# Prompt attention scores with their sign turned and read from pairs of PSUM banks

## The chip, the cores and the metric

The kernel runs on one core of one Trainium2 chip. The metric is the device time of one execution in microseconds; before the change it is 2411.74 us (median of 3 runs, 2409.42 to 2413.18). The core's engines each run their own queue in a fixed order: TensorE (PE; its weight loads are shown apart as PEld), VectorE (DVE), ScalarE (ACT), GpSimd (POOL) and SyncE (SP), which issues most transfers.

## The reference, cut to what matters

The reference is a two-layer encoder step. Layer 0 runs latent attention (8 heads) and a state-space layer side by side, layer 1 is a gated convolution. The change concerns the attention of the prompt alone: 2048 tokens, 16 blocks of 128 queries, and a mask by chunks of 64 tokens.

```python
q_n = rms_norm(q[..., :NOPE_DIM], g_q_nope)                 # 64 columns, scaled by the norm weight
q_r = rope(rms_norm(q[..., NOPE_DIM:], g_q_rope), pos)      # 32 columns
s = (einsum('bqhd,bkhd->bhqk', q_n, k_n) + einsum('bqhr,bkr->bhqk', q_r, k_r)) * ATTN_SCALE
s = where(mask, s, -1e30)        # key chunk <= query chunk
p = softmax(s, axis=-1)
return einsum('bhqk,bkhd->bqhd', p, v)
```

ATTN_SCALE is 96 to the power -0.5; the kernel calls it ATT.

## The kernel before

The program has four stages, one after the other: input projections with the state-space scan (`phase_a`), queries, keys and values with the sample's attention (`phase_b`), the prompt's attention (`phase_c`), and the output projection with layer 1 (`phase_d`). All matmuls that need precision are done in three passes on split operands (high part and low part: `qh`, `ql`, `kh`, `kl`).

In `phase_b`, `p_tr` transposes normalised queries on TensorE; ScalarE copies them out of PSUM (line 702) and multiplies each of the 96 rows by a column `g_qn2`. Its first 64 rows hold the norm weight (times 8, line 445), the other 32 rows hold ones. The result goes to DRAM as `s_qT` and is loaded again per head in `phase_c`.

`phase_c` has 128 steps: 8 heads, and per head 16 blocks `b` of 128 queries. Block `b` sees nk = 128(b+1) keys. A step has these parts:

- **Scores** (`scores`): the keys are cut into chunks of up to 512 columns. Each chunk is three matmuls into one PSUM bank `s_ps` (lines 1301 to 1303). The mask comes in by 16 extra rows of `kh` and `qh`, which add -1e30 to masked scores. VectorE then reads the bank once (line 1304): it copies the scores to SBUF (`s_sb`, or `s_sm` up to 1024 keys) and takes the running maximum of the row, which each following read of the step takes as its operand. The profile shows each read as two rows, the read and a `DVE_READ_ACCUMULATOR`, which writes the maximum.
- **Softmax**: after the last chunk VectorE multiplies the maximum by -ATT (line 1307), ScalarE takes exp(ATT x score + that bias) in one or two pieces and sums (line 1315), VectorE adds the two sums and takes the reciprocal (1318, 1319), GpSimd scales the row (1323).
- **Transposition** (`trans`): groups of up to four 128x128 transpositions fill one PSUM bank `pt` (line 1342); ScalarE copies the bank to `pth` (1351), VectorE writes the rest to `ptl` (1352), and the bank is free.
- **Output** (`av`): per 128 keys two matmuls, with `pth` and `ptl`, into a bank `o` (1362, 1363); after two pairs of blocks `fin` gates and stores the result.

PSUM has eight banks: in this stage two for `o`, three for `pt`, three for `s_ps` (lines 1244 to 1246).

The order of the work is first written out by hand: each piece gets a time by a plan (`cum`, `spread`, lines 1388 to 1460), with scores 8 units ahead of transpositions, and pieces are emitted in order of these times. The context of line 2013 is opened with `schedule_with_timeline_sim=True`; it lays down each engine's order before the run, and this order is not the emitted one: in the trace TensorE takes a transposition of the first step before the second score chunk of the sixth, which was emitted earlier. On the chip the order is fixed, and each engine waits where its next instruction isn't ready.

Of the kernel before, what the change touches and what calls it, by code (L numbers as in the profile page):

```python
# [10 lines left out]
F32 = mybir.dt.float32  # L11
# [3 lines left out]
AF = mybir.ActivationFunctionType  # L15
OP = mybir.AluOpType
# [9 lines left out]
ATT = (64 + 32) ** -0.5  # L26
# [3 lines left out]
PSUM = bass.MemoryType.PSUM  # L30
# [6 lines left out]
def f(ap):  # L37
    return ap.bitcast(F32)
# [22 lines left out]
class K:  # L61
# [362 lines left out]
    def phase_b(self):  # L424
        nc, A, S = self.nc, self.A, self.S
        tt = nc.vector.tensor_tensor
        act = nc.scalar.activation
        with ExitStack() as es:
# [3 lines left out]
            pt = self.pool(es, "b_pt", 2, PSUM)  # L432
            ps = self.s5p
# [8 lines left out]
            for nm, r in (("g_kn2", 128), ("g_qn2", 64), ("g_q64", 128)):  # L442
                t = cp.tile([128, 1], F32, name=nm)
                nc.sync.dma_start(t, A[nm])
                nc.gpsimd.tensor_scalar(t[:r], t[:r], 8.0, 1.0, op0=OP.mult, op1=OP.mult)
                setattr(self, nm, t)
            e3 = cp.tile([128, G, 24], F32, name="e3")
            nc.gpsimd.memset(e3, 64 * EPS)
# [190 lines left out]
            with ExitStack() as e2:  # L639
# [4 lines left out]
                box, nm = {}, {}  # L644
# [593 lines left out]
    def phase_c(self):  # L1238
        nc, A, S = self.nc, self.A, self.S
        with ExitStack() as es:  # L1240
# [1 line left out]
            sp = self.pool(es, "c_s", 2)  # L1242
            kps = (self.kx, self.pool(es, "c_k", 1))
            po = self.pool(es, "c_po", 2, PSUM)
            pt = self.pool(es, "c_pt", 3, PSUM)
            ps = self.pool(es, "c_ps", 3, PSUM)
            hd = {}
            kq = [{nm: kp.tile([112 if nm[1] == "h" else 96, TP], F32R, name=nm) for nm in ("kl", "ql", "kh", "qh")} for kp in kps]
            eye = self.ident[96:112, 96:112][:, :, None].to_broadcast([16, 16, 64])
            for t in kq:  # L1250
                for nm, at, val in (("kh", 1, -1e30), ("qh", 0, 1.0)):
                    r = t[nm][96:112].rearrange("p (b e t) -> p b e t", e=2, t=64)
                    nc.gpsimd.tensor_scalar(r[:, :, at], eye, val, 1.0, op0=OP.mult, op1=OP.mult)
                    nc.gpsimd.tensor_scalar(r[:, :, 1 - at], eye, 0.0, 1.0, op0=OP.mult, op1=OP.mult)
# [27 lines left out]
            def halves(h, nm, c0, first=False):  # L1282
# [4 lines left out]
                else:  # L1287
                    nc.gpsimd.tensor_scalar(hi, f(lo), 1.0, 1.0, op0=OP.mult, op1=OP.mult)
                    nc.gpsimd.tensor_tensor(lo, f(lo), f(hi), op=OP.subtract)

            def scores(h, b):
                t = hd[h]
                nk = 128 * (b + 1)
                sb = sp.tile([128, TP if nk > 1024 else 1024], F32, name="s_sb" if nk > 1024 else "s_sm", bufs=4)
                st = sp.tile([128, 16], F32, name="s_st", bufs=6)
                q = slice(b * 128, b * 128 + 128)
                items = []

                def chunk(i, k0, n, last):
                    o = ps.tile([128, 512], F32, name="s_ps")  # L1300
                    nc.tensor.matmul(o[:, :n], t["qh"][:, q], t["kh"][:, k0:k0 + n], start=True, stop=False)  # L1301
                    nc.tensor.matmul(o[:, :n], t["ql"][:, q], t["kh"][:96, k0:k0 + n], start=False, stop=False)  # L1302
                    nc.tensor.matmul(o[:, :n], t["qh"][:96, q], t["kl"][:, k0:k0 + n], start=False, stop=True)  # L1303
                    nc.vector.tensor_scalar(sb[:, k0:k0 + n], o[:, :n], 1.0, st[:, i - 1:i] if i else None,  # L1304
                                            op0=OP.mult, op1=OP.max, accum_out=st[:, i:i + 1])
                    if last:
                        nc.vector.tensor_scalar(st[:, 5:6], st[:, i:i + 1], -ATT, None, op0=OP.mult)  # L1307
                        e0 = 0
                        parts = []
                        while e0 < nk:  # L1310
                            m = nk - e0
                            m = m if m <= 1024 else 1024 if m > 1152 else 640
                            j = 8 + len(parts)
                            parts.append(j)
                            nc.scalar.activation(sb[:, e0:e0 + m], sb[:, e0:e0 + m], AF.Exp, bias=st[:, 5:6], scale=ATT, accum_out=st[:, j:j + 1])  # L1315
                            e0 += m
                        if len(parts) == 2:
                            nc.vector.tensor_tensor(st[:, 8:9], st[:, 8:9], st[:, 9:10], op=OP.add)
                        nc.vector.reciprocal(st[:, 7:8], st[:, 8:9])  # L1319
                        e0 = 0  # L1320
                        while e0 < nk:
                            m = min(1024, nk - e0)
                            nc.gpsimd.tensor_scalar(sb[:, e0:e0 + m], sb[:, e0:e0 + m], st[:, 7:8], 1.0, op0=OP.mult, op1=OP.mult)  # L1323
                            e0 += m

                k0, i = 0, 0
                while k0 < nk:
                    n = nk - k0
                    if n > 512:
                        n = 384 if n == 640 else 512  # L1330
                    items.append((0.42 * n / 512 * 1.55, lambda i=i, k0=k0, n=n, l=k0 + n == nk: chunk(i, k0, n, l)))
                    k0 += n
                    i += 1
                return sb, items

            def trans(b, sb, pth, ptl):
# [72 lines left out]
                return run  # L1409

            def nchunks(b):
                nk, n = 128 * (b + 1), 0
                while nk > 0:
                    nk -= nk if nk <= 512 else 384 if nk == 640 else 512
                    n += 1
                return n

            def mk_s(n):
                h, a, b = steps[n]

                def make():
                    st_["sb", n], items = scores(h, b)
                    return items
                return make
# [26 lines left out]
            for n, (h, a, b) in enumerate(steps):  # L1451
                t0, t1 = cum[n], cum[n + 1]
                if n % 16 == 0:
                    add(cum[max(0, n - 14)] - LEAD - 4 if n else -1e9, lambda h=h: load(h))
                    if n:
                        spread(cum[n - 9] - LEAD, cum[n - 2] - LEAD, 8, lambda i, h=h: halves(h, "kq"[i % 2], 512 * (i // 2)))
                spread(t0 - LEAD - (t1 - t0), t0 - LEAD, nchunks(b), sub(("S", n), mk_s(n)))
                spread(t0, t1, (b + 4) // 4, sub(("T", n), mk_t(n)))
                if b % 2 == 1:
                    spread(t1 + AVD, t1 + AVD + (t1 - cum[n - 1]), 2 * a + 2, sub(("A", n), mk_a(n, (n // 2) % 2, None)))  # L1460
# [568 lines left out]
```

## Time and profile before

| what | us |
|---|---|
| median of 3 runs | 2411.74 |
| the profiled execution | 2409.65 |
| its span in the trace | 2407.9 |
| PE, busy in the span | 2228.1 (93%) |
| PEld | 2006.6 (83%) |
| DVE | 1834.1 (76%) |
| POOL | 1427.4 (59%) |
| ACT | 1177.0 (49%) |

An engine is busy while an instruction of it runs; starts of the next may lie under the end of one. The span runs from the first to the last instruction of the trace. The prompt's attention lies in the middle of it, from about 0.9 to 1.4 ms. "Idle before, releaser" says what ended the time in which an engine stood still; a wait of PEld is a wait before a weight load, which is the first instruction of a matmul.

### The profile page before, as it was taken

How to read it: one execution, taken by the hardware profiler on the slowest of the kernel's cores; microseconds unless marked ns; L12 is line 12 of the kernel's file. 1: busy time of each engine (PE TensorE's matmuls, PEld its weight loads, DVE VectorE, ACT ScalarE, POOL GpSimd, SP SyncE). 2: the span in 40 equal slices, each digit the busy share in tenths (PEclk: the TensorE clock that was granted, in tenths of full speed). 3: DMA queues.
4: the chain of work that ended last, by engine and by line, in shares of the span. 5: the costliest groups of instructions: out<-in, count | busy, mean ns of one | idle time of the engine just before them, and what ended most of it. 6: DMA issues, size and time to landing. Idle time of an engine off the chain costs nothing.

```text
span 2407.9 us, 39063 instructions
## 1 busy us (share of the span) xinstructions
PE 2228.1 (93%) x13471; PEld 2006.6 (83%) x13471; DVE 1834.1 (76%) x3995; ACT 1177.0 (49%) x2226; POOL 1427.4 (59%) x1328
## 2 busy tenths in 40 slices
PE   6798989998889987999999989999999999999996
PEld 6798989996648876888888888988888789989996
DVE  7763246985456666888889945999998999999984
ACT  4343346235436765777777743433433533533423
POOL 5232543216265666777777534686778888976851
PEclk9999999999989987999999999999999999999998
DMA  8886574315637772222222356755355245443552
GB/s 193 200 222 160 133 187 148 93 49 167 198 109 217 229 238 78 71 65 72 71 73 67 97 198 201 245 180 166 120 171 172 85 140 206 153 141 121 159 166 86
DMA packets 289670, 352.08 MB, mean 146 GB/s; under 512 B 79936, under 2 KB 231808, under 8 KB 288960
## 3 DMA queue, kind: packets, MB, share of 16 engines
q1 hardware_dynamic: 288768, 348.40, 48.8%
q8 instruction: 107, 1.75, 0.3%
q10 hardware_dynamic: 704, 1.18, 0.2%
q14 instruction: 91, 0.75, 0.1%
HBM read 255.72 MB, written 93.52 MB: 145 GB/s over the span
## 4 chain that ended last, share of the span: by engine, by line
PE 50%; DVE 6%; POOL 2%; ACT 2%; DMA 2%; issue 1%; SPq 0%; POOLq 0%; DVEq 0%; ACTq 0%
PE pp L71 12%; PE pp L72 12%; PE pp L73 12%; PE pt L1342 4%; PE o L1363 2%; PE o L1362 2%; PE s_ps L1301 2%; PE s_ps L1302 2%; PE s_ps L1303 2%; DVE acc L1652 1%; DVE s_sb L1304 1%; DVE ptl L1352 1%; ACT s_sb L1315 1%; DMA b1l<-s_mx_l 1%; DMA ql<-s_qT 1%
## 5 line engine op out<-in xcount | busy, mean ns | idle before, releaser
L1652 DVE SCALAR_TENSOR_TENSOR acc<-vt,cw,acc 128x384 f32<-128x384 f32 (+2 forms) x1142 | 670.0, 659 | 2.5 <-ACT acc L1638 1.3
L1848 POOL TENSOR_TENSOR wl<-wr,wh 128x1024 fp32r<-128x1024 f32 x110 | 265.7, 2417 | 113.3 <-ACT wh L1847 112.3
L1847 ACT ACTIVATE wh<-wr 128x1024 fp32r<-128x1024 f32 x136 | 144.1, 1060 | 327.8 <-PE pp L72 161.9
L1352 DVE TENSOR_TENSOR ptl<-pt,pth 128x512 fp32r<-128x512 f32 (+2 forms) x320 | 184.3, 601 | 20.1 <-ACT pth L1351 18.7
L1351 ACT ACTIVATE pth<-pt 128x512 fp32r<-128x512 f32 (+2 forms) x320 | 158.7, 527 | 67.3 <-PE pt L1342 65.2
L71 PE MATMUL pp<-b0h,wh 128*128 128x512 f32 (+1 forms) x488 | 181.2, 371 | 7.1 <-ACT b0h L1755 6.0
L72 PE MATMUL pp<-b0l,wh 128*128 128x512 f32 (+1 forms) x488 | 181.1, 371 | 0.0
L73 PE MATMUL pp<-b0h,wl 128*128 128x512 f32 (+1 forms) x488 | 180.5, 370 | 0.0
L1848 POOL TENSOR_TENSOR w<-wr,w 128x1024 fp32r<-128x1024 f32 x57 | 137.5, 2412 | 65.0 <-ACT w L1847 59.5
L71 PE MATMUL pp<-xh,vh 128*128 128x256 f32 (+1 forms) x448 | 134.7, 301 | 30.3 <-ACT vh L192 10.8
L1847 ACT ACTIVATE w<-wr 128x1024 fp32r<-128x1024 f32 x64 | 67.8, 1060 | 186.7 <-PE pp L72 106.1
L1323 POOL TENSOR_SCALAR s_sb<-s_sb,s_st 128x1024 f32<-128x1024 f32 (+7 forms) x128 | 118.5, 938 | 62.7 <-DVE s_st L1319 20.7
L1363 PE MATMUL o<-ptl,v 128*128 128x256 f32 x576 | 148.9, 297 | 0.0
L1362 PE MATMUL o<-pth,v 128*128 128x256 f32 x576 | 146.6, 283 | 2.2 <-ACT pth L1351 2.2
L1301 PE MATMUL s_ps<-kh,qh 112*128 112x512 f32 (+3 forms) x320 | 131.1, 411 | 11.7 <-DVE s_sm L1304 5.2
L73 PE MATMUL pp<-xh,vl 128*128 128x256 f32 (+1 forms) x448 | 132.8, 297 | 1.7 <-DVE mx L209 1.7
L72 PE MATMUL pp<-xl,vh 128*128 128x256 f32 (+1 forms) x448 | 133.2, 297 | 0.0
L71 PE MATMUL pp<-xh,wh 128*128 128x256 f32 (+1 forms) x384 | 114.8, 299 | 16.4 <-ACT qsum L230 11.5
L1315 ACT ACTIVATE s_sb<-s_sb,s_st 128x1024 f32<-128x1024 f32 (+6 forms) x128 | 122.0, 956 | 16.1 <-DVE s_st L1307 15.2
L1342 PE MATMUL pt<-ident,s_sb 128*128 128x128 f32 x800 | 118.6, 275 | 6.9 <-DVE ptl L1352 3.4
L1302 PE MATMUL s_ps<-kh,ql 96*128 96x512 f32 (+3 forms) x320 | 118.7, 371 | 0.0
L1303 PE MATMUL s_ps<-kl,qh 96*128 96x512 f32 (+3 forms) x320 | 118.0, 369 | 0.0
(515 smaller groups left out, 7587.7 us busy)
## 6 DMA issues: line engine op xcount, KB each, us to landing
wr<-w_c SPq DMA_DIRECT2D x120, 512.0 KB, 3.5
wr<-w_o SPq DMA_DIRECT2D x80, 512.0 KB, 3.6
raw<-xT SPq DMA_DIRECT2D x28, 512.0 KB, 4.9
raw<-x SPq DMA_DIRECT2D x16, 512.0 KB, 6.0
s_v<-v_hl SPq DMA_DIRECT2D x8, 1024.0 KB, 6.4
tb<-s_x SPq DMA_DIRECT2D x32, 256.0 KB, 3.4
raw<-w_m SPq DMA_DIRECT2D x15, 512.0 KB, 6.8
v<-s_v SPq DMA_DIRECT2D x15, 512.0 KB, 4.8
```

The source lines that it names most:

```text
L71: mm(o, wh, xh, start=first, stop=False)
L72: mm(o, wh, xl, start=False, stop=False)
L73: return mm(o, wl, xh, start=False, stop=last)
L1301: nc.tensor.matmul(o[:, :n], t["qh"][:, q], t["kh"][:, k0:k0 + n], start=True, stop=False)
L1302: nc.tensor.matmul(o[:, :n], t["ql"][:, q], t["kh"][:96, k0:k0 + n], start=False, stop=False)
L1342: nc.tensor.transpose(p[:, i, :], sb[:, (c + i) * 128:(c + i + 1) * 128], self.ident)
L1352: nc.vector.tensor_tensor(ptl[:, c:c + m, e:e + 128], p[:, :m, :], f(pth[:, c:c + m, e:e + 128]), op=OP.subtract)
L1362: nc.tensor.matmul(w, v[:, c, :], pth[:, c, lo:], start=c == 0, stop=False)
L1363: nc.tensor.matmul(w, v[:, c, :], ptl[:, c, lo:], start=False, stop=c == 2 * a + 1)
L1652: stt(box[i], vt[:, k:k + n], cw[:, ct, k:k + 1], src, op0=OP.mult, op1=OP.add)
L1847: act(h, r, AF.Copy)
L1848: (nc.vector if vec_split(slots[i]) else nc.gpsimd).tensor_tensor(l, r, f(h), op=OP.subtract)
```

## The change

Queries carry the sign and the scale: `g_qn2` is multiplied by -8 ATT in its norm-weight rows and by -ATT in the others, so the score matmuls give -ATT x score. The mask adds +1e30. The running maximum becomes a running minimum, which serves as the bias of the exponential as it is (scale -1), and line 1307 is gone.

Scores are written into tiles of two PSUM banks. A step's keys are cut by `pieces`: full pairs of 512 + 512, then the rest, in one bank if it is at most 512, else as two equal halves in two banks. VectorE reads once per piece, after its last matmul, up to 1024 columns. `pt` goes from three banks to two, `s_ps` from three tiles of one bank to two tiles of two. The number of chunks per step, and with it the plan of pieces, stays as it was.

```diff
-                nc.gpsimd.tensor_scalar(t[:r], t[:r], 8.0, 1.0, op0=OP.mult, op1=OP.mult)
+                nc.gpsimd.tensor_scalar(t[:r], t[:r], -8.0 * ATT if nm == "g_qn2" else 8.0, 1.0, op0=OP.mult, op1=OP.mult)
+                if nm == "g_qn2":
+                    nc.gpsimd.tensor_scalar(t[64:], t[64:], -ATT, 1.0, op0=OP.mult, op1=OP.mult)
...
-            pt = self.pool(es, "c_pt", 3, PSUM)
-            ps = self.pool(es, "c_ps", 3, PSUM)
+            pt = self.pool(es, "c_pt", 2, PSUM)
+            ps = self.pool(es, "c_ps", 2, PSUM)
...
-                for nm, at, val in (("kh", 1, -1e30), ("qh", 0, 1.0)):
+                for nm, at, val in (("kh", 1, 1e30), ("qh", 0, 1.0)):
...
+            def pieces(b):
+                nk = 128 * (b + 1)
+                out = [(512, 2)] * (nk // 1024)
+                r = nk % 1024
+                return out + ([(r, 1)] if 0 < r <= 512 else [(r // 2, 2)] if r else [])
...
-                def chunk(i, k0, n, last):
-                    o = ps.tile([128, 512], F32, name="s_ps")
-                    nc.tensor.matmul(o[:, :n], t["qh"][:, q], t["kh"][:, k0:k0 + n], start=True, stop=False)
-                    nc.tensor.matmul(o[:, :n], t["ql"][:, q], t["kh"][:96, k0:k0 + n], start=False, stop=False)
-                    nc.tensor.matmul(o[:, :n], t["qh"][:96, q], t["kl"][:, k0:k0 + n], start=False, stop=True)
-                    nc.vector.tensor_scalar(sb[:, k0:k0 + n], o[:, :n], 1.0, st[:, i - 1:i] if i else None,
-                                            op0=OP.mult, op1=OP.max, accum_out=st[:, i:i + 1])
+                def part(i, j, k0, n, m):
+                    if j == 0:
+                        box["o"] = ps.tile([128, 2, 512], F32, name="s_ps")
+                    o = box["o"][:, j, :n]
+                    k = k0 + n * j
+                    nc.tensor.matmul(o, t["qh"][:, q], t["kh"][:, k:k + n], start=True, stop=False)
+                    nc.tensor.matmul(o, t["ql"][:, q], t["kh"][:96, k:k + n], start=False, stop=False)
+                    nc.tensor.matmul(o, t["qh"][:96, q], t["kl"][:, k:k + n], start=False, stop=True)
+                    if j < m - 1:
+                        return
+                    last = k + n == nk
+                    nc.vector.tensor_scalar(sb[:, k0:k0 + n * m].rearrange("p (m n) -> p m n", m=m), box["o"][:, :m, :n], 1.0, st[:, i - 1:i] if i else None,
+                                            op0=OP.mult, op1=OP.min, accum_out=st[:, i:i + 1])
                     if last:
-                        nc.vector.tensor_scalar(st[:, 5:6], st[:, i:i + 1], -ATT, None, op0=OP.mult)
...
-                            nc.scalar.activation(sb[:, e0:e0 + m], sb[:, e0:e0 + m], AF.Exp, bias=st[:, 5:6], scale=ATT, accum_out=st[:, j:j + 1])
+                            nc.scalar.activation(sb[:, e0:e0 + m], sb[:, e0:e0 + m], AF.Exp, bias=st[:, i:i + 1], scale=-1.0, accum_out=st[:, j:j + 1])
```

## Rows read from the trace of the kernel before

**Rows 1.** Windows of the attention: each engine's busy us (instructions), clock, DMA share, GB/s.

```profile
922.30:1404.80 482.50, 462.87 (x3163) 414.68 (x3163) 421.58 (x1297) 362.73 (x760) 335.59 (x351) 0.99 0.25 68
```

**Rows 2.** Timeline of PE: start, us, line, out<-in, shape, count.

```profile
1182.60 0.28 PE L1362 MATMUL o<-pth,v 128*128 128x256 f32 x1
1182.72 0.28 PE L1363 MATMUL o<-ptl,v 128*128 128x256 f32 x1
```

**Rows 3.** Waits of weight loads in the attention: us in total, times, longest.

```profile
PEld pt L1342 <- POOL s_sm L1323: 10.9, 12, 1.6
PEld s_ps L1301 <- DVE s_sb L1304: 8.3, 22, 1.2
PEld pt L1342 <- POOL s_sb L1323: 6.4, 8, 1.8
PEld pt L1342 <- DVE ptl L1352: 5.1, 10, 0.7
PEld o L1362 <- ACT pth L1351: 3.1, 3, 2.2
...
PEld s_ps L1301 <- DVE s_sm L1304: 1.7, 4, 0.5
```

**Rows 4.** Chain of waits in the attention, shares by line.

```profile
by line: PE pt L1342 18.8%; PE o L1363 10.1%; PE o L1362 9.9%; PE s_ps L1301 9.2%; PE s_ps L1302 8.3%; PE s_ps L1303 8.1%; DVE s_sb L1304 5.6%; issue 5.0%; DVE ptl L1352 4.6%; ACT s_sb L1315 3.8%; POOL o_t L1375 2.4%; POOL ql L1289 1.9%; AC
```

**Rows 5.** Groups by line and shape, VectorE: count, busy us, mean ns, idle before.

```profile
L1304 DVE TENSOR_SCALAR_CACHE_REDUCE s_sb<-s_ps,s_st 128x512 f32<-128x512 f32 x96 | 71.5, 745 | 10.0 <-PE s_ps L1303 7.2
L1304 DVE TENSOR_SCALAR_CACHE_REDUCE s_sb<-s_ps 128x512 f32<-128x512 f32 x64 | 43.6, 682 | 4.1 <-PE pt L1342 3.3 <-PE s_ps L1303 0.6
...
L1307 DVE TENSOR_SCALAR s_st<-s_st 128x1 f32<-128x1 f32 x128 | 17.5, 144 | 0.4
...
L1304 DVE TENSOR_SCALAR_CACHE_REDUCE s_sb<-s_ps,s_st 128x256 f32<-128x256 f32 x32 | 15.2, 474 | 0.4
...
L1304 DVE DVE_READ_ACCUMULATOR s_sb<-s_ps,s_st 128x1 f32 x160 | 12.9, 81 | 0.0
```

**Rows 6.** Timeline of VectorE, reads that follow one another.

```profile
1143.35 0.15 DVE L1307 TENSOR_SCALAR s_st<-s_st 128x1 f32<-128x1 f32 x1
1143.41 0.68 DVE L1304 TENSOR_SCALAR_CACHE_REDUCE s_sb<-s_ps 128x512 f32<-128x512 f32 x1
1144.02 0.09 DVE L1304 DVE_READ_ACCUMULATOR s_sb<-s_ps 128x1 f32 x1
1144.22 0.75 DVE L1304 TENSOR_SCALAR_CACHE_REDUCE s_sb<-s_ps,s_st 128x512 f32<-128x512 f32 x1
1144.90 0.08 DVE L1304 DVE_READ_ACCUMULATOR s_sb<-s_ps,s_st 128x1 f32 x1
1145.10 0.75 DVE L1304 TENSOR_SCALAR_CACHE_REDUCE s_sb<-s_ps,s_st 128x512 f32<-128x512 f32 x1
```

**Rows 7.** Chain of waits, one bank's life: start us, us, what, count.

```profile
1103.22 0.45 PE pt L1342 x4
...
1103.70 0.61 ACT pth L1351
...
1104.33 0.70 DVE ptl L1352
...
1105.07 0.66 PE pt L1342 x4
```

**Rows 8.** The transposition tile: count, duration ns min/median/max, first and last start, forms.

```profile
L1352 DVE TENSOR_TENSOR ptl<-pt,pth x320: 264/676/693, 925.4 to 1404.1; 128x512 fp32r<-128x512 f32 x128, 128x128 fp32r<-128x128 f32 x16, 128x384 fp32r<-128x384 f32 x16
L1342 PEld LDWEIGHTS pt<-ident,s_sm x288: 137/140/231, 922.3 to 1361.9; 128*128 128x128 f32 x144
```

**Rows 9.** Waits of ScalarE: us in total, times, longest.

```profile
ACT s_sb L1315 <- DVE s_st L1307: 15.2, 20, 1.7
ACT s_sm L1315 <- DVE s_st L1307: 14.7, 12, 1.6
```

**Rows 10.** Line 445, set-up on GpSimd: duration ns, first and last start.

```profile
L445 POOL TENSOR_SCALAR g_qn<-g_qn x1: 352/352/352, 541.2 to 541.2; 64x1 f32<-64x1 f32 x1
```

More of the change, by code (lines that the diff above doesn't have):

```diff
@@ L1289, in halves @@
                     nc.gpsimd.tensor_tensor(lo, f(lo), f(hi), op=OP.subtract)
+            def pieces(b):
[3 more added lines that the diff above has]
+                return out + ([(r, 1)] if 0 < r <= 512 else [(r // 2, 2)] if r else [])
             def scores(h, b):
+                box = {}
                 t = hd[h]
@@ L1324, in chunk @@
                             e0 += m
[L1326 to L1333, printed above, removed]
+                k0 = 0
+                for i, (n, m) in enumerate(pieces(b)):
+                    for j in range(m):
+                        items.append((0.0, lambda i=i, j=j, k0=k0, n=n, m=m: part(i, j, k0, n, m)))
+                    k0 += n * m
                 return sb, items
@@ L1411, in nchunks @@
             def nchunks(b):
[L1412 to L1416, printed above, removed]
+                return sum(m for _, m in pieces(b))
             def mk_s(n):
```

## The prediction

> **What bounds the kernel now.** I read the windows first. The prompt attention, from its first transposition to its last, is the stretch 922.3 to 1404.8 us. In its 482.5 us TensorE is busy 462.87 us, VectorE 421.58, ScalarE 362.73 and GpSimd 335.59, at a granted clock of 0.99 [rows 1]. So the edit falls into one stretch where two engines are nearly full. The reader is not to take 462.87 for a full TensorE: the timeline shows `o` matmuls that last 0.28 us and start 0.11 to 0.12 us apart, so the end of each lies under the next [rows 2]. What really stands still is better seen in the waits of the weight loads: for the normalised scores from GpSimd 10.9 and 6.4 us, for the score reads on VectorE 8.3 and 1.7, for a transposition bank that VectorE has not yet emptied 5.1, for `pth` 3.1 [rows 3]. These six make 35.5 us, 7% of the stretch. The chain of waits says the same: 64.4% of it are TensorE's six lines, 10.2% the two VectorE lines (score reads 5.6%, `ptl` 4.6%), 5.0% issue, 3.8% the exponentials [rows 4]. TensorE sets the end; VectorE, with PSUM between them, is what holds it up.
>
> **Part 1: fewer and wider reads.** Per head the score chunks stay 40 (320 in all, as many as now), so the matmuls are unchanged in number and columns: nothing. The reads fall from 320 to 192: a pair is read at once wherever a step's remainder is over 512 columns. A read with the running statistic as its operand takes 745 ns for 512 columns, 474 for 256: 1.06 ns a column and 203 ns fixed; its accumulator read adds 81 [rows 5]. 128 such reads go, their columns stay: 128 x (203 + 81) = 36.4 us. The bias multiply goes too, 128 x 144 ns = 18.4 us [rows 5]. Together 54.8 us, 13% of VectorE's 421.58. This is the upper figure, since ends overlap: a first read is followed 0.61 us after its start. Where two reads of one row follow each other, the second starts 0.20 us after the accumulator read of the first began [rows 6], so there a merged pair saves 0.88 - 0.54 = 0.34 us. So VectorE gets back some 26 us (only starts counted: 128 x 0.14, and 128 x 0.06 for the bias multiply) to 52 us (128 x 0.34 + 8).
>
> A read of 1024 columns is not in the trace. From below it costs its columns, 1.09 us; from above two reads, 1.49. I take 1.22: 682 ns for a first read of 512 plus 512 x 1.06 [rows 5].
>
> What of that reaches the end? Not VectorE's time, but what TensorE waits for: the score reads, 8.3 + 1.7 = 10.0 us [rows 3]. I let these go: -10. The bounds are 0 (the work freed lies beside TensorE's) and -35.5 (every wait of rows 3 goes). What is late next is GpSimd's normalising, 17.3 us, which the edit leaves alone.
>
> The Trainium skill weighs this both ways ("Perfetto Trace Analysis", Optimizing Scalar/DVE Operations): larger operations help a saturated engine, but an engine that is not saturated and still makes others wait is better served by smaller ones. VectorE's 87% here lies between the two; by the first sentence the freed time comes back (the first rival), by the second the wider reads cost (the third).
>
> **Part 2: one transposition bank less.** This is what the wider reads are paid with. `pt` has three banks and gets two. The chain shows the shortest life of a bank: transpositions at 1103.22, copy to `pth` 0.61 us, subtraction to `ptl` 0.70, and the next group of four starts in the freed bank at 1105.07: 1.85 us [rows 7]. 320 groups go through in 482.5 us, one per 1.51 us; with three banks a bank comes round every 4.52 us, with two every 3.02. From the first weight load of each group to the end of its `ptl` (320 pairs in order, the first 922.3 to 925.7, the last 1402.7 to 1404.8; lines L1342 and L1352 in [rows 8]) I get a mean life of 3.10 us. That is more than 3.02, before any time that a freed bank waits for TensorE. In the same records all three banks are in use 35% of the time, two or more 76%; and 162 of the 320 groups begin before the `ptl` of the group two before them has ended, by 1.02 us on average, 166 us in sum. In today's order these 162 starts would be late.
>
> Not all of it is lost. The order of each engine is drawn up anew for two banks, there are `o` matmuls to put in front, and lives will shrink, as VectorE has less queued. So the price lies between 0 (lives fall below 3.02 less a wait, and the order absorbs the rest) and 166. The trace gives 0.5 us as a typical wait of this kind (5.1 us in 10 places [rows 3]). I let one in four of the 162 places keep such a wait: 40 x 0.5 = +20.
>
> A rule speaks for a price here: in the Trainium skill ("Perfetto Trace Analysis", Identifying Performance Opportunities) gaps that repeat on the engine that should be full can mean too little PSUM for the next tile. The trace agrees so far as TensorE waits for `ptl` even with three banks.
>
> **Part 3: scores in two pairs instead of three banks.** A bank of scores is taken by the first of a chunk's three matmuls and freed by the read. From the first weight load to the end of the read the 320 banks live 3.63 us on average, so 2.4 of 3 are taken, 80%. A pair also waits for its second chunk (1.51 us) and its read is 0.5 us longer; 128 pairs at 3.63 + 2.0 less today's queueing behind reads that go (some 1 us) = 4.6, and 64 singles at 3.6 less 1: 3.9 on average. A buffer comes round every 2 x 482.5 / 192 = 5.0 us: 78%. The same: 0. If today's queueing stays it is 98%, and some of the 10 us of part 1 stays with it.
>
> **Part 4: the way from scores to probabilities.** ScalarE waits 15.2 us (20 times) for the bias multiply before exponentials of `s_sb` and 14.7 us (12 times) before those of `s_sm` [rows 9]. Those waits don't vanish: the running statistic is ready where the multiply now starts, 0.15 us earlier. Against it, a tail of two chunks (64 of 128 steps) ends with a read 1.22 - 0.75 = 0.47 us longer. TensorE waits for the normalised scores 20 times on its weight loads (12 + 8 [rows 3]); half of them with +0.32, half with -0.15: +2. Bounds: -3 (20 x 0.15) and +6 (20 x 0.32).
>
> **Part 5: the rest.** The sign and the scale go into the multiplication of the query transposition, which already takes a per-row scale: 0. One more column operation on GpSimd at set-up is like the existing one, 0.35 us [rows 10], beside other work. The mask's sign costs nothing. No DMA is added or moved.
>
> **Sum.** -10 + 20 + 0 + 2 = +12 on the profiled execution's 2409.65: 2421.7. That execution lies 2.1 us under the median of the runs, 2411.74, so the forecast against the median is 2424.
>
> **Rivals.**
> First, faster: VectorE is the real limit. For it: it is busy 87%, its chained reads leave 0.20 us holes [rows 6], and the waits for `ptl` and for score reads are its doing. If lives of `pt` banks fall with its queue to about 2.6 us, two banks are enough, and half of the 26 to 52 us freed comes back: -20, 2392. Against it: TensorE has only 35.5 us to win, half of that GpSimd's. It decides at the mean life of a bank: under about 2.7 us this one, above 2.9 the forecast.
> Second, no change: the 10 us of part 1 and a pool price of the same size cancel (one in eight late places), or the new order hides both: 2412.
> Third, clearly slower: the wide read is no cheaper than two (1.49 us), VectorE keeps its load, and a `ptl` that comes ready behind a read waits up to 1.2 us instead of 0.75. Then lives stay at 3.10, a freed bank waits on average half a score matmul more, 0.2 us, and 320 x 3.30 / 2 = 528 us would be needed; part of it hidden by the new order leaves some +35: 2447.
>
> **How the numbers follow.** What counts as no change is 0.2%, 4.8 us, about what a measurement of this kernel can tell. Forecast (+5 to +25, 2417 to 2437): 0.40. First rival 0.32. Second 0.18. Third 0.10. So faster 0.32, same 0.18, slower 0.50. The range of 8 in 10 runs into the first rival down to 2393, which leaves out about one in eight, and into the third up to 2446. The forecast's own range is 2417 to 2437.
>
> **What would show it.** Right: 192 reads instead of 320, the 1024-column one near 1.22 us, VectorE's busy time in the stretch down by about 55 us; weight loads of transpositions waiting for `ptl` up from 5.1 us to 20 or more, waits for score reads gone or small; the stretch 490 to 505 us long; the rest of the span as before within a few us. Wrong: the waits for `ptl` stay near 5 us and the stretch is under 478 us; then VectorE was the limit. Wrong in another way: reads of 1024 near 1.5 us, or a difference that lies outside this stretch, since the order is drawn up for the whole program.

## The result and the profile after

The changed kernel takes 2483.39 us (median of 4 runs, 2478.58 to 2491.03) against 2410.97 of the kernel before: ratio 1.0297, 95% interval 1.0277 to 1.0316. It is slower by 72 us, where +12 was forecast and 2446 was the upper end. The profiled execution took 2478.58 us, its span is 2476.8.

All of the loss is in the stretch from the first transposition to the last `ptl`, now 914.9 to 1478.4 us: 563.5 us, where it was 482.5 [rows 1]. That is +81.0; the rest of the span is 12.1 us shorter. The window of that stretch, columns as in [rows 1]:

```profile
914.90:1478.40 563.50, 493.71 (x3180) 429.08 (x3179) 417.33 (x925) 371.87 (x767) 335.59 (x353) 0.98 0.22 59
```

The clock is 0.98 (0.99 before): TensorE runs at 1.2 GHz instead of 2.4 for 24.1 us of the stretch, 14.0 before, and the 10 us added at half the clock cost at most 5. TensorE and ScalarE run as many instructions as before to within 1%: their same work takes 81 us more. The chain of waits, shares by line:

```profile
by line: PE pt L1353 14.2%; PE s_ps L1313 8.4%; DVE s_sb L1319 7.7%; PE o L1373 7.0%; issue 6.9%; PE o L1374 6.8%; PE s_ps L1314 6.5%; PE s_ps L1315 6.4%; ACT pth L1362 5.3%; DVE ptl L1363 5.2%; ACT s_sb L1329 5.0%; POOL s_sb L1337 2.6%; DV
```

TensorE's six lines fall from 64.4% [rows 4] to 49.3%; the reads, `ptl`, the exponentials and issue rise, and so do the copies to `pth`, under 2% before. The waits name the places (us in total, times, longest; PE rows are waits before a matmul, PEld before a weight load):

```profile
ACT pth L1362 <- PE pt L1353: 124.2, 145, 3.0
...
DVE ptl L1363 <- ACT pth L1362: 65.4, 96, 1.7
ACT s_sb L1329 <- DVE s_sb L1319: 41.3, 28, 2.1
PEld s_ps L1313 <- DVE s_sb L1319: 34.4, 42, 1.9
...
PE pt L1353 <- DVE ptl L1363: 26.2, 54, 1.1
DVE s_sb L1319 <- PE pt L1353: 26.2, 24, 1.5
...
PE s_ps L1313 <- DVE s_sb L1319: 24.3, 31, 1.6
...
PEld pt L1353 <- issue: 14.9, 25, 1.4
...
PEld pt L1353 <- DVE ptl L1363: 14.0, 18, 1.4
PEld o L1373 <- ACT pth L1362: 13.3, 23, 1.1
```

The same view of the kernel before, beside [rows 3]:

```profile
ACT pth L1351 <- PE pt L1342: 65.2, 78, 2.8
...
DVE ptl L1352 <- ACT pth L1351: 18.7, 35, 2.0
...
PE pt L1342 <- DVE ptl L1352: 3.4, 10, 0.6
PE s_ps L1301 <- DVE s_sb L1304: 3.4, 7, 0.9
DVE s_sb L1304 <- PE pt L1342: 3.3, 5, 1.0
```

Two things are to be seen. TensorE waits for `ptl`, 14.0 us on weight loads (5.1 before [rows 3]) and 26.2 on matmuls (3.4 before). And it waits for score reads far more than before, though there are fewer of them: 34.4 us on weight loads of `s_sb` alone, 8.3 before. Meanwhile the engines that empty the banks stand idle: ScalarE 124 us waiting for transpositions (65.2 before), VectorE 65 us in `ptl` waiting for `pth` (18.7 before). They wait on each other in a ring: bank, `pth`, `ptl`, bank.

These rows can't be added up. In the records all 54 waits before matmuls follow a weight load that waited for the same bank, so they show its wait a second time. And the 25 waits that the profile puts down to issue end 0.12 us after the `ptl` that frees the bank, so they are waits for it too. Counted once, as weight loads that stood for more than 0.15 us and began within 0.13 us of the `ptl` that freed their bank, TensorE waits 66 times for a transposition bank, 42.2 us in all; before it was 20 times and 9.7 us. Its weight loads wait 44.8 us for score reads, 10.0 before. What these two have grown by makes 67 of the 81 us.

VectorE's reads by shape, columns as in [rows 5]:

```profile
L1363 DVE TENSOR_TENSOR ptl<-pt,pth 128x512 fp32r<-128x512 f32 x224 | 152.1, 684 | 59.9 <-ACT pth L1362 57.4
L1319 DVE TENSOR_SCALAR_CACHE_REDUCE s_sb<-s_ps 128x1024 f32<-128x1024 f32 x64 | 77.9, 1218 | 28.2 <-PE pt L1353 26.2 <-PE s_ps L1315 1.7 <-POOL s_sb L1337 0.2
...
L1319 DVE TENSOR_SCALAR_CACHE_REDUCE s_sb<-s_ps,s_st 128x1024 f32<-128x1024 f32 x8 | 10.2, 1273 | 0.0
```

The wide read costs what was forecast, 1.218 us (1.22). Reads and accumulator reads together sum to 193.4 us against 230.6, 37 us less, and the bias multiply is gone. Yet VectorE's busy time hardly moves, 421.58 to 417.33. Busy is the time in which at least one instruction runs: the durations in the stretch sum to 503.1 us before and 467.7 after, and 81.5 us of them lay under one another before, 50.4 now. VectorE waits more than before, and its instructions overlap less.

One place in the timeline shows the ring (start, us, engine, line; in brackets idle time and releaser):

```profile
1203.71 0.39 PE L1313 MATMUL s_ps<-kh,qh 112*128 112x512 f32 x1
...
1204.88 0.40 PE L1315 MATMUL s_ps<-kl,qh 96*128 96x512 f32 x1
...
1204.90 0.08 DVE L1319 DVE_READ_ACCUMULATOR s_sm<-s_ps 128x1 f32 x1
1204.90 0.55 DVE L1363 TENSOR_TENSOR ptl<-pt,pth 128x384 fp32r<-128x384 f32 x1
...
1205.40 0.62 PE L1353 MATMUL pt<-ident,s_sm 128*128 128x128 f32 x4
...
1206.07 0.60 ACT L1362 ACTIVATE pth<-pt 128x512 fp32r<-128x512 f32 x1
...
1206.16 1.23 DVE L1319 TENSOR_SCALAR_CACHE_REDUCE s_sm<-s_ps 128x1024 f32<-128x1024 f32 x1 [0.70 <-PE pt L1353]
...
1207.38 0.67 DVE L1363 TENSOR_TENSOR ptl<-pt,pth 128x512 fp32r<-128x512 f32 x1
```

A pair is complete at 1205.28. VectorE is free at 1205.45 but stands 0.70 us, until transpositions of an earlier step have read the SBUF row that the read is to fill. The read of 1.23 us then holds up `ptl`, whose `pth` was ready at 1206.67, until 1207.38. One bank lives 2.7 us, one pair 3.7.

### The profile page after: what moved, and what is told of

Same layout as the page of the kernel before. It is cut to its first block, busy times and chain, and to the rows that moved or that the text cites. A ratio compares the mean times of both kernels' runs of the same rounds, so it can differ in the third digit from the quotient of the medians.

```text
span 2476.8 us, 38557 instructions
## 1 busy us (share of the span) xinstructions
PE 2247.1 (91%) x13471; PEld 2010.5 (81%) x13471; DVE 1830.6 (74%) x3611; ACT 1184.5 (48%) x2226; POOL 1423.1 (57%) x1329
## 4 chain that ended last, share of the span: by engine, by line
PE 48%; DVE 5%; POOL 4%; ACT 4%; DMA 2%; issue 2%; DVEq 0%; SPq 0%; POOLq 0%; ACTq 0%
PE pp L71 12%; PE pp L73 12%; PE pp L72 12%; PE pt L1353 3%; PE s_ps L1313 2%; DVE s_sb L1319 2%; PE o L1373 2%; PE o L1374 2%; PE s_ps L1314 1%; PE s_ps L1315 1%; ACT pth L1362 1%; DVE ptl L1363 1%; ACT s_sb L1329 1%; DMA b1l<-s_mx_l 1%; POOL s_sb L1337 1%
## 5 line engine op out<-in xcount | busy, mean ns | idle before, releaser
L1363 DVE TENSOR_TENSOR ptl<-pt,pth 128x512 fp32r<-128x512 f32 (+2 forms) x320 | 189.3, 604 | 68.0 <-ACT pth L1362 65.4
L1362 ACT ACTIVATE pth<-pt 128x512 fp32r<-128x512 f32 (+2 forms) x320 | 163.7, 529 | 126.0 <-PE pt L1353 124.2
L1313 PE MATMUL s_ps<-kh,qh 112*128 112x512 f32 (+4 forms) x320 | 131.5, 411 | 33.4 <-DVE s_sb L1319 24.3
L1353 PE MATMUL pt<-ident,s_sb 128*128 128x128 f32 x800 | 126.6, 280 | 29.1 <-DVE ptl L1363 26.2
L1353 PEld LDWEIGHTS pt<-ident,s_sb 128*128 128x128 f32 x800 | 92.1, 143 | 45.8 <-issue 14.7
L1373 PEld LDWEIGHTS o<-pth,v 128*128 128x128 f32 x576 | 110.5, 192 | 15.4 <-ACT pth L1362 13.3
```

What stands on the lines that cost most here:

```text
L1313: nc.tensor.matmul(o, t["qh"][:, q], t["kh"][:, k:k + n], start=True, stop=False)
L1353: nc.tensor.transpose(p[:, i, :], sb[:, (c + i) * 128:(c + i + 1) * 128], self.ident)
L1362: nc.scalar.activation(pth[:, c:c + m, e:e + 128], p[:, :m, :], AF.Copy)
L1363: nc.vector.tensor_tensor(ptl[:, c:c + m, e:e + 128], p[:, :m, :], f(pth[:, c:c + m, e:e + 128]), op=OP.subtract)
L1373: nc.tensor.matmul(w, v[:, c, :], pth[:, c, lo:], start=c == 0, stop=False)
```

## The experiments

In the table at the end, life is the mean time from a group's first weight load to the end of its `ptl`, free the mean time from there to the first weight load of the group that takes the same bank; both are worked out from the records of the 320 groups, as the 3.10 us of the prediction. Their sum is a bank's round, and by construction the stretch is 160 rounds with two banks, 107 with three: the two say where a bank's time goes, not why. "Bank" is what TensorE waits for a transposition bank, counted once as above. "Reads" and `pth` are what it waits for these, PE and PEld rows of the stretch together; a wait can stand in both rows, so these columns serve to compare kernels. "1.2 GHz" is the time of the stretch in which TensorE had the lower of its two clocks. All are in us.

**The sign alone** (three banks each, narrow reads):

```diff
-                nc.gpsimd.tensor_scalar(t[:r], t[:r], 8.0, 1.0, op0=OP.mult, op1=OP.mult)
+                nc.gpsimd.tensor_scalar(t[:r], t[:r], -8.0 * ATT if nm == "g_qn2" else 8.0, 1.0, op0=OP.mult, op1=OP.mult)
...
-                        nc.vector.tensor_scalar(st[:, 5:6], st[:, i:i + 1], -ATT, None, op0=OP.mult)
```

> The sign and scale in the queries alone: no bias multiply (128 VectorE instructions fewer), chunks, reads and banks as before. Theory A (the missing transposition bank costs the time) and theory B (two pairs of score banks, read late and at once, cost the time) both expect little: 2404 to 2414 us. A rival that the turned sign itself or the rescaled queries cost the time expects 2430 or more.

Ratio 0.9962 (0.994 to 0.9984), 2399.82 us: a small gain, and faster than both kernels.

**One transposition bank less, nothing else:**

```diff
-            pt = self.pool(es, "c_pt", 3, PSUM)
+            pt = self.pool(es, "c_pt", 2, PSUM)
```

> The kernel before with two transposition banks instead of three, all else as it was. Theory A: most of the 72 us, 2455 to 2485. Theory B: the price I had put on this bank at most, 2411 to 2435. Theory C (both together feed a loop: late transpositions keep the score rows in SBUF taken, these hold the reads, the reads hold the score banks): 2411 to 2440, far less than the whole.

Ratio 1.0167 (1.0135 to 1.0199): +40 us by the bank alone. Its waits:

```profile
PE pt L1342 <- DVE ptl L1352: 23.7, 53, 3.4
PEld pt L1342 <- DVE ptl L1352: 19.3, 30, 1.2
PEld pt L1342 <- issue: 17.9, 41, 3.5
```

All 53 waits of the first row follow a weight load that waited for the same bank, and 40 of the 41 of the last end 0.12 us after their bank is freed. Counted once, 96 weight loads wait for their bank, 0.53 us on average, 50.5 us in all; before there were 20, 9.7 us. The 76 added ones make 41 us, about what the run loses.

**The sign with two transposition banks**, score banks as before (the two edits above together):

> Sign and scale in the queries, two transposition banks, three single score banks: seven banks in all, one left empty. Theory A (the missing transposition bank is the cause, nearly alone): like the run with the sign and four score banks, 2460 to 2475, so that the fourth score bank is worth nothing. Theory D (a fourth score bank makes it worse, as scores run further ahead and push VectorE's other work back): the 40 us of the missing bank on top of 2400, so 2435 to 2450.

Ratio 1.0225 (1.0192 to 1.0258): 2.6% over the sign alone, 63 us. So most of what the whole change loses is here already, with narrow reads of single banks. The next two runs lie between 1.0225 and 1.0297, and their intervals don't part the fourth score bank from the pairs and their reads.

The clock has a share in the 63 us. The windows of the stretch with the sign alone and with the sign and two banks, columns as in [rows 1]:

```profile
912.70:1391.00 478.30, 458.23 (x3167) 411.44 (x3167) 417.88 (x1179) 366.77 (x767) 336.46 (x353) 0.99 0.26 70
...
918.10:1459.80 541.70, 490.16 (x3174) 424.64 (x3174) 431.71 (x1179) 371.61 (x767) 336.19 (x353) 0.96 0.23 61
```

TensorE is at 1.2 GHz for 9.2 us of the first and 38.2 us of the second (before 14.0, with the bank alone 15.2). The 29 us added at half the clock cost at most half of that, 14 us, an estimate from these times. Why the clock is lower here is open: it was 0.91 from 970 to 1020 us with TensorE busy for 43.82 us, and 1.00 from 1170 to 1220 us with 43.59.

**The same with the freed bank as a fourth single score bank:**

```diff
-            ps = self.pool(es, "c_ps", 3, PSUM)
+            ps = self.pool(es, "c_ps", 4, PSUM)
```

> Sign and scale in the queries, two transposition banks, and the four score banks of the change used singly, with the narrow reads of before. Theory A: like e2, 2450 to 2485. Theory B: the time is in the pairing, so near before or under it, 2400 to 2425. Theory C: 2405 to 2440, as four single banks don't need both halves free.

Ratio 1.0261 (1.023 to 1.0293). The waits for reads are nearly gone, 7.6 us, and the kernel is not faster: those for a transposition bank are 59.8 us.

**The whole change, each bank of a pair read by itself:**

```diff
-                    if j < m - 1:
-                        return
...
+                    nc.vector.tensor_scalar(sb[:, k:k + n], o, 1.0, st[:, i - 1:i] if i else None,
```

> The change, but each bank of a pair is read for itself right after its chunk; only the pair is freed as a whole. The reads are 320 again. Theory A: what the late wide read costs is small, 2465 to 2495, as the change. Theory B (the late read of 1024 columns that holds VectorE and both banks is a good part of it): 2440 to 2462.

Ratio 1.0272 (1.0243 to 1.0301). From the whole change (1.0297, 1.0277 to 1.0316) it can't be told apart: with two transposition banks the wide read wins nothing that these runs can measure.

**Four transposition banks, two score banks** (with the sign):

```diff
-            pt = self.pool(es, "c_pt", 3, PSUM)
-            ps = self.pool(es, "c_ps", 3, PSUM)
+            pt = self.pool(es, "c_pt", 4, PSUM)
+            ps = self.pool(es, "c_ps", 2, PSUM)
```

> The trade turned round: sign and scale in the queries, four transposition banks, two single score banks. Theory A: transposition banks are what is short, scores are not: 2385 to 2405. Rival (score banks are short too, as 80% of three are in use): 2410 to 2450, and TensorE waits for score reads instead.

Ratio 1.01 (1.0072 to 1.0129). `ptl` is waited for twice in all, 0.9 us, and now the score side is short. Neither side has a bank to spare; three and three is the best split that was run. The clock has a share here too, with 45.9 us of the stretch at 1.2 GHz. The waits:

```profile
PEld s_ps L1303 <- DVE s_sb L1306: 22.2, 42, 1.7
...
PEld s_ps L1303 <- DVE s_sm L1306: 17.8, 24, 3.9
```

**Wide reads with three transposition banks, first try:** one tile of three score banks, used as pair and single in turn.

```diff
-            ps = self.pool(es, "c_ps", 3, PSUM)
+            ps = self.pool(es, "c_ps", 1, PSUM)
+            ring, pos = ps.tile([128, 3, 512], F32, name="s_ps"), [0]
```

> Wide reads without paying with a transposition bank: three of those, and three score banks as a ring, in which two neighbouring free banks are read together and the third alone. Theory A: below the kernel with the sign alone, 2380 to 2400, as VectorE gets back part of its time and nothing is taken away. Theory B (a wide read that holds two of three banks to its end stalls the scores): 2410 to 2450.

Ratio 1.0701 (1.0669 to 1.0734). It doesn't test what it was meant to: the three banks, as one tile, wait for one another like a single buffer. In the records no piece's first weight load begins before the read of the piece before it has ended. The clock of the stretch falls to 0.88, which is part of the price.

```profile
PEld s_ps L1305 <- DVE s_sb L1310: 70.9, 75, 2.6
...
PE s_ps L1305 <- DVE s_sb L1310: 48.9, 57, 2.3
```

**Second try:** a tile of two banks and a tile of one, in turn; `pt` keeps three.

```diff
-                    o = ps.tile([128, 512], F32, name="s_ps")
+                    if j == 0:
+                        box["o"] = ps.tile([128, 1 if p else 2, 512], F32, name="s_p1" if p else "s_p2")
```

> Sign turned, transpositions keep three banks; the three score banks are one tile of two banks and one of one bank, used in turn, so that a step's scores are read in pieces of up to 1024 and up to 512 columns: fewer reads without the lost transposition bank. If VectorE's freed time is worth something to this stage, 2380-2398. If the score side needs three buffers that come free one by one, 2425-2500, with the waits of score matmuls for reads well above the 10 us of the kernel before.

Ratio 1.0005 (0.9987 to 1.0022), neither of the two outcomes expected: no slower than before, but slower than the sign alone with narrow reads.

```profile
PEld s_p L1309 <- DVE s_sb L1314: 17.7, 23, 1.7
DVE ptl L1365 <- ACT pth L1364: 17.0, 37, 1.7
...
PE s_p L1309 <- DVE s_sb L1314: 11.1, 17, 1.3
...
PEld s_p L1309 <- DVE s_sm L1314: 8.1, 8, 4.7
...
PEld pt L1355 <- DVE ptl L1365: 5.1, 7, 0.9
```

The waits for a transposition bank are back to 9.9 us and VectorE's wait for `pth` to 17.0; what is left are reads, 42.8 us against 16.0 of the sign alone. Two things differ from the sign alone: the reads are wider (255 instead of 320), and three score banks that came free one by one are now a pair and a single. The clock can be up to 6 of the 10 us between the two, by 21.9 us at 1.2 GHz against 9.2.

**Emptying first:** the two instructions of `grp` get priority when the orders are laid down, with the sign and two banks, with the sign and three, and with the whole change.

```diff
+                    with self.tc.high_priority():
                         nc.scalar.activation(pth[:, c:c + m, e:e + 128], p[:, :m, :], AF.Copy)
```

> Sign turned, two transposition banks, three single score banks, narrow reads, and the two instructions that empty a transposition bank (to pth and to ptl) given priority when each engine's order is drawn up, so that they stand ahead of score reads and exponentials wherever they can. Without the priority 1.0225, mean life of a bank 2.83 us, 0.54 us from its release to the next group's first weight load. If the price of the lost bank comes from the emptying being queued behind other work (a long life), the life falls to about 2.3 us and the time to 2425-2450. If it comes from TensorE's fixed order (a freed bank waits until TensorE comes back to a transposition), the life falls but the time that a free bank waits rises, and the time stays at 2455-2475.

> Sign turned with three banks each (0.9962 without the priority), and the same priority for the emptying of the transposition banks. If lives of banks still cost TensorE time with three banks, 2385-2396. If three banks are enough as they are, 2396-2406, as without the priority. If the exponentials and score reads that are put back cost more than the banks win, over 2406.

> The whole change, and priority for the emptying of the transposition banks when the orders are drawn up. If the change loses because the emptying comes late behind reads of 1.2 us and exponentials, 2430-2460, with the wait of the pth copies and of ptl well down. If it loses because two banks with TensorE's fixed order are too few, 2470-2490 as before.

Ratios 1.0237 (1.0201 to 1.0272), 0.9966 (0.9946 to 0.9985), 1.0316 (1.0293 to 1.0339): each as without the priority. But with two banks, and in the whole change, the orders are the same: every instruction of TensorE, VectorE, ScalarE and GpSimd, by tile, operation and shape, stands where it stood without the priority (3867 of VectorE with two banks), and the life is 2.84 us where it was 2.83. So the edit changed nothing there and tests neither case: whether earlier emptying would pay for the bank stays open. What these pairs show is how close two kernels of one order come: 1.0225 and 1.0237, 1.0297 and 1.0316.

**A fifth long score row in SBUF** (three short ones for room), in the whole change and in the sign alone:

```diff
-                sb = sp.tile([128, TP if nk > 1024 else 1024], F32, name="s_sb" if nk > 1024 else "s_sm", bufs=4)
+                sb = sp.tile([128, TP if nk > 1024 else 1024], F32, name="s_sb" if nk > 1024 else "s_sm", bufs=5 if nk > 1024 else 3)
```

> The whole change, with five SBUF score rows for long steps in place of four (and three for short ones in place of four, for room). If the score reads are held because score rows come free late, their wait for transpositions (26 us in 24 places) goes, TensorE's waits for reads fall from 75 us by at least 20, and the time falls to 2455-2470. If they stand behind ptl on VectorE, which waits for a copy of a bank that came late, the waits stay and the time is 2475-2492.

> The sign turned alone (0.9962), with five long and three short score rows. With three transposition banks rows come free early enough: 2394-2408 if rows are not short here. Under 2392 if a fifth row helps by itself, over 2412 if the short steps need their fourth row.

Ratios 1.03 (1.0263 to 1.0337) and 1.0052 (1.0031 to 1.0072). By time alone the first theory fell, and the second kernel came out as its last case had it, in which the short steps miss their fourth row. The traces part the two effects: the edit shortens the stretch of the changed kernel, 563.5 to 549.4 us, and lengthens that of the sign alone, 478.3 to 488.7; the stage behind it is longer by 17 and 12 us in the two, which takes the gain away (why is not settled). Waits of the changed kernel with five rows:

```profile
DVE ptl L1363 <- ACT pth L1362: 85.7, 101, 4.1
...
PE pt L1353 <- DVE ptl L1363: 34.8, 57, 2.5
PEld pt L1353 <- issue: 27.0, 37, 2.9
...
PE s_ps L1313 <- DVE s_sb L1319: 12.0, 23, 0.7
PEld s_ps L1313 <- DVE s_sb L1319: 11.4, 20, 0.7
...
DVE s_sb L1319 <- PE pt L1353: 4.4, 6, 0.8
```

The wait for rows falls from 26.2 to 4.4 us, and TensorE's for reads from 74.9 to 38.8, as the first theory had it. Of these 36 us the stretch keeps 14: the waits for a transposition bank rise from 42.2 to 57.8, and the time at 1.2 GHz from 24.1 to 37.8.

All in one table:

| kernel | ratio | stretch | life | free | waits: bank (times) | reads | `pth` | 1.2 GHz |
|---|---|---|---|---|---|---|---|---|
| before | 1 | 482.5 | 3.10 | 1.41 | 9.7 (20) | 14.2 | 5.3 | 14.0 |
| sign | 0.9962 | 478.3 | 3.06 | 1.39 | 10.2 (28) | 16.0 | 3.6 | 9.2 |
| sign, wide reads, three banks | 1.0005 | 495.0 | 3.03 | 1.56 | 9.9 (22) | 42.8 | 1.8 | 21.9 |
| two banks | 1.0167 | 522.0 | 2.66 | 0.60 | 50.5 (96) | 22.9 | 9.8 | 15.2 |
| sign, two banks | 1.0225 | 541.6 | 2.83 | 0.54 | 55.3 (78) | 33.1 | 9.5 | 38.2 |
| the same, four score banks | 1.0261 | 547.1 | 2.67 | 0.74 | 59.8 (81) | 7.6 | 30.7 | 34.1 |
| whole change, two reads | 1.0272 | 550.9 | 2.66 | 0.76 | 36.7 (69) | 62.5 | 17.4 | 25.7 |
| whole change | 1.0297 | 563.5 | 2.85 | 0.65 | 42.2 (66) | 74.9 | 20.7 | 24.1 |
| whole change, five rows | 1.03 | 549.4 | 2.59 | 0.82 | 57.8 (76) | 38.8 | 8.1 | 37.8 |

All rows with two banks lie between 1.0167 and 1.03, all with three at or near 1; each has an order of its own, so this is not the luck of one order. Among the rows with two banks, what TensorE is seen to wait for changes far more (bank 36.7 to 59.8 us, reads 7.6 to 74.9) than the time does.

## Why the prediction was wrong

The sign was right: slower, by the lost bank. The size was not.

**Part 2 is the step that failed**, and the -10 of part 1 with it. "I let one in four of the 162 places keep such a wait: 40 x 0.5 = +20." The size of the wait was right, 0.53 us with the bank alone; the count was not, and no row stood behind it: 96 weight loads wait for their bank where 20 did before, 76 more and not 40. 76 x 0.53 is 40 us, and the run shows +40. In the whole change 46 more wait, for longer, 33 us in all, and the waits for reads take another 35 us, where part 1 had them gone. The count was too low because the late starts were thought to be absorbed by a new order and by shorter lives. Lives did fall, to 2.59 to 2.85 us, below the 3.02 that two banks allow. But a round is longer than a life: a freed bank lies for 0.54 to 0.82 us on average before TensorE, in its fixed order, begins the next group in it. With the bank alone 123 of 318 groups begin within 0.13 us of the release, and the others 0.9 us after it on average. So the round is 3.26 us there (2.66 + 0.60) and 3.50 in the whole change, where 3.02 would have kept the time: 0.24 and 0.48 us too long, 160 times. With three banks a freed bank lay for 1.41 us, and 40 groups began within 0.13 us of the release. The third rival priced just this time, but at 0.2 us.

For the same reason the test between forecast and first rival, a mean life under 2.7 us, was a wrong one: four kernels of the table are under it and slower by 1.7 to 3.0%. Life and free time together make the round.

**Part 1** was right in VectorE's instructions (37 us less in reads, 36.4 forecast; a read of 1.218 us) and wrong in what comes of them. It let TensorE's 10.0 us of waits for reads go, -10; in the whole change its weight loads wait 44.8 us for them. With three transposition banks wide reads cost some +10: they move the ratio from 0.9962 to 1.0005, and TensorE's waits for reads from 16.0 to 42.8 us, though the regrouping of the score banks and the clock are in this as well. Fewer and wider reads bought no time in any run. Here the second of the two sentences that the prediction weighed, in the Trainium skill ("Perfetto Trace Analysis", Optimizing Scalar/DVE Operations), fits: an engine that is not saturated but makes others wait may do better with smaller instructions. The trace agrees, by those 42.8 us. With two transposition banks no difference shows: two reads for one give 1.0272 against 1.0297.

**Part 3** said 78% of the score tiles in use, cost 0, or 98% with today's queueing, which it did not expect to stay. From the records a score tile lives for 5.2 us on average, where 3.9 was forecast and 4.9 makes the 98%; over the longer stretch that is 89% of two pairs. The queueing stayed, with 74.9 us of waits for reads. Rows in SBUF that come free late add to it, as the experiment with five rows showed; the prediction had not looked at them. But removing those waits did not bring the time back while `pt` had two banks: with four single score banks only 7.6 us of them are left, at 1.0261, and the waits for a transposition bank are longer instead.

**Part 4** put +2 on the way from scores to probabilities, within bounds of -3 and +6. The sign alone gives -0.4% (9 us), but without the longer last read that the +2 came from; what part 4 cost within the whole change no run separates. **Part 5** held as far as seen.

Of the signs named, 192 reads and 1.22 us came as said. Weight loads waiting for `ptl`, forecast at 20 us or more, came as 14.0 in the row that names it and as 42.2 with those that stand under other names; the waits for score reads grew instead of vanishing; the stretch is 563.5 us, not 490 to 505; the rest of the span, said to stay within a few us, is 12.1 us shorter; VectorE's busy time did not fall by 55, as its overlap went. The first two rivals fell. The third was nearest in time (2447) with the wrong cause in its first half: the wide read is cheaper than two.

Open: why the sign makes the lost bank dearer (63 against 40 us). By the estimate above the lower clock can be up to 14 of these 23 us. The orders are laid down anew for each kernel, and no run here separates that from the edit. Whole pairs with three transposition banks, paid for by a bank of `o`, have no time: with a single bank of `o` the program ended in a deadlock before it could run. So this direct test of whole pairs against the lost bank is missing.

## What to carry to other kernels

Before giving up a buffer, count in the trace the starts that would come too early without it, and take none of them off without a row that says why. Here 162 of 320 starts would have been late, 40 were priced as waits, and 76 came. A mean life that fits into the buffers left is not enough, since the time that a buffer lies free until the engine in its fixed order comes back to it counts as well. That time can't be carried over from the kernel before: with three banks the round was 4.51 us, with two 3.26. A wider instruction on an engine that isn't the limit won nothing here, and the waits for the buffers that it holds until its end grew. The waits of a profile tell where a ring of engines stops, not which of its links is short: change one link at a time, as here one bank. And count a wait once: it can stand before the weight load, again before the matmul, or under issue.

## What the runs showed that was not expected

A read of 1024 columns across two banks takes 1.218 us (1.273 with the running statistic as operand), close to the columns of two and the fixed cost of one. Three banks taken as one tile behave as one buffer: 1.0701, with 190.5 us of waits for reads. VectorE's busy time stood still (4 us less) while the durations of its instructions fell by 35 us, because the overlap went too. Waits that the profile puts down to issue, 17.9 us before transpositions with the bank alone, were waits for the bank in 40 of 41 cases.
